# Moving the mLSTM gates behind the second projection, and opening two more products of the output projection at the mLSTM's end

## The chip, the cores and the metric

The kernel runs on one core of a Trainium2 chip. The metric is the device time of one execution in microseconds (us). Before the change it is 1308.25 us, the median of three runs from 1307.04 to 1308.48.

## The reference

One layer of an encoder over 512 tokens of width 1024, in float32:

- RMSNorm and one input projection, whose columns feed three mixers side by side: pooling with four windows; a bidirectional mLSTM with 4 heads of width 64; attention with 8 query heads and 2 key/value heads. Their outputs, 1024 columns together, go through one output projection and are added to x.
- In the mLSTM, q and k pass a convolution over 5 tokens and a SiLU. Each token has an input gate and a forget gate per head and direction. Running sums of the log forget gates and running maxima give decays; a head's scores q k are multiplied by the decays, and the values are summed with them. The two directions are added, normed per head and multiplied with a sigmoid of another projection.
- RMSNorm, then cross-attention (4 heads) into 256 memory tokens, added to x.
- RMSNorm, then 16 experts with SwiGLU, each taking its 64 best tokens, added to x; a last RMSNorm.

## The kernel before

The 512 tokens stand as 4 tiles of 128 (t = 0 to 3), the 1024 columns as 8 blocks of 128. A float32 product outside the experts is made from three faster ones: both factors are split into a high and a low part (`split`, L129 to L136: ScalarE casts the high part, VectorE or GpSimd subtracts), and `mm3` (L124 to L127) issues high x high, high x low and low x high. So a projection block with 8 steps is 24 products.

PSUM has eight banks, used by name: three for "mm", one for "oo", two for "tr" (transposes) and two for "sc" (scores). A name's banks go round in the order in which the program asks for them: a tile waits until the tile that held its bank has been read.

Work is written as generators that yield a cost after each piece. `weave(chain, filler, ratio)` (L161) emits a piece of the chain, multiplies its cost by the ratio, and emits pieces of the filler until that is paid; `run` emits what is left. This gives the order of the program. The framework then places the instructions (it is built with `schedule_with_timeline_sim=True`), and each engine executes its own queue in the order so found, which can differ from the order of the program where operands are ready earlier.

Stages around the change, in order:

1. The first half of attention (heads 0 to 3, `att_0`) is woven with two projections ("og", "vo"). Then `turn` (L355) transposes the queries of the second half.
2. The second half, `attention(4, 8)`, is the chain of a weave at ratio 1.0, and `fill_m` (L580) is its filler: the projection "mq" with its convolution, the load of "pl" (`load_w(7)`), `gates()`, the projection "mk" with its convolution, the decays of head 0 in both directions, the load of "k0" (`load_w(8)`). The attention chain has 21.2 units of cost, "mq" and "mk" 10.24 each.
3. `gates` (L593 to L639) works on tiles of 32 columns. It takes five "mm" tiles: one for the running sums (L610 to L612), two for transposes of `az` (L628), read by scans on VectorE (L630, L632), and two to turn the scans back (L636), read at L637. `az` lies in memory that the first half of attention used; GpSimd clears it at L622. `decay` takes one "mm" tile (L656), which ScalarE reads four times (L659).
4. `mlstm` is the chain of the next weave, at ratio 1.4, with `fill_kv` as its filler: the pool projection "pl", the pooling, the keys and values of the cross-attention ("k0", "k1", "v0", "v1"), and then three tiles of the output projection: (0,0), (1,0) and (0,1), as (token tile, half of the columns). These three take the "mm" banks and are held open: six of their eight steps are issued (`korder[:6]`), because the last two need the mLSTM's output. The filler has 44.0 units in all, the chain 31.9. At the end of head 1 and of head 3 stands a norm, a row of VectorE instructions (L760 to L765) with one on ScalarE; `out_turn` (L706) then turns two heads' result and splits it for the output projection.
5. `out_proj(0)` finishes the tiles of t = 0 and 1, adding each to x (L913): the held ones with their last two steps, (1,1) with all eight. `out_proj(1)` does t = 2 and 3 as the filler of the cross-attention's queries. The weights of these queries are split (L135, L136) into memory that is free after the turn.
6. The cross-attention, the routing and the experts follow. Each of the 16 experts has 24 MB of weights, read in pieces by `issue` into every arena of SBUF that the earlier stages have freed.

Of the kernel before, what the change touches and what calls it, by code (L numbers as in the profile page):

```python
# [98 lines left out]
def build(nc, tc, A, out, ne=NE, dbg=None):  # L99
# [21 lines left out]
    def SC():  # L121
        return ps.tile([128, 512], F32, name="sc")
# [91 lines left out]
    def load_w(i, parts=2):  # L214

        if i >= len(plan):
            return
        name, src, c0, n = plan[i]
        hb, lb = wring.next(), wring.next()
        st = KT // parts  # L220
        for j in range(parts):
            a, b = j * st, (j + 1) * st
            rbuf = raw.next()
            SP.dma_start(rbuf.f[:, 0:st, :n], src[:, a:b, c0:c0 + n])
            split(rbuf.f[:, 0:st, :n], hb.f[:, a:b, :n], lb.f[:, a:b, :n], le=(G if j % 2 and i < 7 else V))
        W[name] = (hb, lb, n)
# [86 lines left out]
    def fm_chunk(w, done):  # L313
        hb, lb, _ = W[w]
        for blk in range(2):
            p = MM()
            for k in range(KT):
                bs = slice(blk * 128, (blk + 1) * 128)
                mm3(p, hb.r[:, k, bs], lb.r[:, k, bs], hT_h[k].r, hT_l[k].r, k == 0, k == KT - 1)
                yield 0.64  # L320
            done(blk, p)
# [77 lines left out]
    fill = fill_q2()  # L399
# [180 lines left out]
    def fill_m():  # L580
        yield from fm_chunk("mq", conv_done(0))
        load_w(7)
        gates()
        yield from fm_chunk("mk", conv_done(1))
        for d in range(2):
            early.append(decay(0, d, MM))
            yield 0.43
        load_w(8)


    gs = Wr = None
# [1 line left out]
    def gates():  # L593
        az = Wr.bufs[0].f[:, 0:1024].rearrange("p (t d c) -> p t d c", d=2, c=128)
        Mrow = [Wr.bufs[1].f[:, d * S:(d + 1) * S] for d in range(2)]
        fpre = gt.f[:, :, 8:16]
        ipre = gt.f[:, :, 0:8]
        nf, ef, lf, bc, ag, mt, em, of = (gs.f[:, i] for i in range(8))
        mk_ = nf
        V.tensor_scalar(nf, fpre, -1.0, None, op0=ALU.mult)  # L600
        V.tensor_tensor(nf, nf, fpre, op=ALU.min)
        C.activation(ef, nf, AF.Exp)
        C.activation(ef, ef, AF.Ln, bias=1.0)
        V.scalar_tensor_tensor(lf, fpre, 0.0, ef, op0=ALU.min, op1=ALU.subtract)

        p = MM()
        pb = p[:, :32].rearrange("p (t c) -> p t c", c=8)
        pc = p[:, 32:64].rearrange("p (t c) -> p t c", c=8)
        F_, B_ = slice(0, 4), slice(4, 8)
        T.matmul(pb[:, :, F_], tri.f[:, 0], lf[:, :, F_], start=True, stop=True)  # L610
        T.matmul(pb[:, :, B_], tri.f[:, 1], lf[:, :, B_], start=True, stop=True)
        T.matmul(pc, ones.f, lf, start=True, stop=True)  # L612
        G.memset(of[:, 0, F_], 0.0)
        G.memset(of[:, 3, B_], 0.0)
        V.tensor_copy(of[:, 1, F_], pc[:, 0, F_])
        V.tensor_copy(of[:, 2, B_], pc[:, 3, B_])
        for i in range(2):
            V.tensor_tensor(of[:, 2 + i, F_], of[:, 1 + i, F_], pc[:, 1 + i, F_], op=ALU.add)
            V.tensor_tensor(of[:, 1 - i, B_], of[:, 2 - i, B_], pc[:, 2 - i, B_], op=ALU.add)
        V.tensor_tensor(bc, pb, of, op=ALU.add)  # L620
        V.tensor_tensor(ag, ipre, bc, op=ALU.subtract)
        G.memset(az, 0.0)  # L622
        V.tensor_copy(az.rearrange("p t d (h z) -> p (t d) h z", z=32)[:, :, :, 0],
                      ag.rearrange("p t (d h) -> p (t d) h", d=2))
        for d in range(2):
            p = MM()
            for t in range(NT):
                T.transpose(p[:, t * 128:(t + 1) * 128], az[:, t, d], idn)  # L628
            if d == 0:
                V.tensor_tensor_scan(Mrow[d], z0, p, 0.0, op0=ALU.max, op1=ALU.max)  # L630
            else:
                V.tensor_tensor_scan(Mrow[d][:, ::-1], z0, p[:, ::-1], 0.0, op0=ALU.max, op1=ALU.max)  # L632
        for d in range(2):
            p = MM()
            for t in range(NT):
                T.transpose(p[:, t * 128:(t + 1) * 128], Mrow[d][:, t * 128:(t + 1) * 128], idn)  # L636
            V.tensor_copy(mk_[:, :, 4 * d:4 * d + 4], p.rearrange("p (t h z) -> p t h z", t=4, z=32)[:, :, :, 0])  # L637
        V.tensor_tensor(mt, mk_, bc, op=ALU.add)
        C.activation(em, mt, AF.Exp, scale=-1.0)  # L639
# [33 lines left out]
    fill = fill_1()  # L673
# [15 lines left out]
    fill = fill_m()  # L689
# [13 lines left out]
    def out_turn(blk):  # L703
        p = OO()
        for t in range(NT):
            T.transpose(p[:, t * 128:(t + 1) * 128], hsum.f[:, t, blk * 128:(blk + 1) * 128], idn)  # L706
        split(p, y_h[2 + blk].f, y_l[2 + blk].f)
        yield 0.43

    def mlstm():  # L710
        nxt = early
        for h in range(4):
            wts = nxt
            if h < 3:
                nxt = [decay(h + 1, d, OO) for d in range(2)]
            for st in range(NT):
                p = SC()
                mm3(p, kz_h[h].r[:, st * 128:(st + 1) * 128], kz_l[h].r[:, st * 128:(st + 1) * 128],
                    mq_h[h // 2].r, mq_l[h // 2].r, True, True)
                for d in range(2):  # L720
                    o, js = seg[d][st]
                    wa = wts[d].f[:, o:o + js.stop - js.start]
                    V.scalar_tensor_tensor(wa, p[:, js], 1.0 / 32.0, wa, op0=ALU.mult, op1=ALU.mult)
                yield 0.64
            yield 1.0
            for d in range(2):
                c = 4 * d + h
                p = TR()
                pv = p[:, :NT * 65].rearrange("p (t c) -> p t c", c=65)
                for t in range(NT):  # L730
                    src = [st for st in range(NT) if (st <= t if d == 0 else st >= t)]
                    for i, st in enumerate(src):
                        o, js = seg[d][st]
                        oo = o + t * 128 - js.start
                        T.matmul(pv[:, t], wts[d].f[:, oo:oo + 128], mv[st].f[:, h, :],  # L735
                                 start=(i == 0), stop=(i == len(src) - 1))
                    yield 0.21 * len(src)
                if h == 2 and d == 1:
                    yield from out_turn(0)
                m = mst.next()  # L740
                dn, rc = m.f[:, 0:4], m.f[:, 4:8]
                V.scalar_tensor_tensor(dn, pv[:, :, 64], -1.0, em[:, :, c], op0=ALU.mult, op1=ALU.max)
                V.tensor_tensor(dn, dn, pv[:, :, 64], op=ALU.max)
                V.reciprocal(rc, dn)
                rb_ = rc[:, :, None].to_broadcast([128, NT, 64])
                ho = hsum.f[:, :, h * 64:(h + 1) * 64]
                if d == 0:
                    V.tensor_tensor(ho, pv[:, :, 0:64], rb_, op=ALU.mult)
                else:
                    tb = htmp.next()  # L750
                    V.tensor_tensor(tb.f[:, :, 0:64], pv[:, :, 0:64], rb_, op=ALU.mult)
                    V.tensor_tensor(ho, ho, tb.f[:, :, 0:64], op=ALU.add)
            if h % 2 == 0:
                continue

            sq, y, tm = (nst.f[:, i, h // 2] for i in range(3))
            tb = htmp.next()
            ho, oh = (b.f[:, :, (h - 1) * 64:(h + 1) * 64] for b in (hsum, og))
            C.activation(tb.f, ho, AF.Square)
            V.tensor_reduce(sq, tb.f.rearrange("p t (h d) -> p (t h) d", d=64), axis=AX.X, op=ALU.add)  # L760
            mean_rsqrt(sq, y, tm, 64)
            V.scalar_tensor_tensor(tb.f.rearrange("p t (h d) -> p t h d", d=64), ho.rearrange("p t (h d) -> p t h d", d=64),
                                   0.5, y.rearrange("p (t h) -> p t h", h=2)[:, :, :, None].to_broadcast([128, NT, 2, 64]),
                                   op0=ALU.mult, op1=ALU.mult)
            V.tensor_tensor(ho, tb.f, oh, op=ALU.mult)  # L765
        yield from out_turn(1)


# [36 lines left out]
    korder = [4, 5, 6, 7, 0, 1, 2, 3]  # L805
    wo_h, wo_l, held = {}, {}, {}
# [71 lines left out]
            yield from out_part(t, c, held[t, c], korder[:6])  # L878

    fill = fill_kv()  # L880
    weave(mlstm(), fill, 1.4)
    run(fill)
    kvT_h, kvT_l = kv["k"]
    vca = kv["v"]
# [219 lines left out]
    fill = out_proj(1)  # L1104
# [33 lines left out]
    fill = fill_q()  # L1138
# [311 lines left out]
```

## Time and profile before

| What | us |
|---|---|
| median of three runs | 1308.25 |
| the profiled execution, its own time | 1307.97 |
| span of that execution, first to last instruction | 1306.3 |
| PE (TensorE matmul) busy | 1236.4 (95%) |
| VectorE (DVE) busy | 441.6 (34%) |
| ScalarE (ACT) busy | 272.2 (21%) |
| GpSimd (POOL) busy | 118.1 (9%) |

The mean granted clock of TensorE is 0.988. In the profile, busy time per slice shows two halves: up to about 400 us several engines work and the DMA engines are far from full; from then on to the end PE and the DMA engines are both at nine tenths or more. Busy PE time is modelled from pipelined matmuls, so that a busy PE is not PE at its peak, and shares over the whole span mix stages with different limits. They are read stage by stage in the rows below.

### The profile page before, as it was taken

What the parts mean: (1) busy time and instruction counts of PE and PEld (TensorE: products, weight loads), DVE (VectorE), ACT (ScalarE), POOL (GpSimd) and SP (SyncE); (2) the same over time, 40 slices, a digit from 0 to 9 for tenths busy, and PEclk for the clock granted to TensorE, in tenths of its full rate; (3) what the DMA queues carried; (4) which work ended last, traced back from release to release, by engine and by line L of the source; (5) the groups of instructions that cost most, each with busy time, mean ns of one, the idle gap of its engine ahead of it and who ended that gap; (6) DMA issues with size and microseconds to landing.
All of it is one profiled execution on the core that took longest, in us unless ns stands there. A gap on an engine that the chain in (4) does not pass through costs nothing.

```text
span 1306.3 us, 15428 instructions
## 1 busy us (share of the span) xinstructions
PE 1236.4 (95%) x6257; PEld 637.5 (49%) x6257; DVE 441.6 (34%) x1007; ACT 272.2 (21%) x577; POOL 118.1 (9%) x157
## 2 busy tenths in 40 slices
PE   9898999899989999999999999999999999999986
PEld 8874779688853443343343334334333433433333
DVE  5897777436750022121221221202113020211313
ACT  6565645324410000101001010000101000010113
POOL 5422442103100000000000000000000000000012
PEclk9999999899989999999999999999999999999998
DMA  8210124305869899999999999999999999999995
GB/s 289 85 50 33 49 70 142 116 33 227 334 240 392 359 427 429 427 424 428 424 428 426 425 428 426 424 427 427 425 428 426 424 427 427 425 425 428 426 407 192
DMA packets 59974, 432.73 MB, mean 331 GB/s; under 512 B 5120, under 2 KB 23168, under 8 KB 30848
## 3 DMA queue, kind: packets, MB, share of 16 engines
q1 hardware_dynamic: 59904, 431.76, 80.4%
q8 instruction: 49, 0.80, 0.2%
q14 instruction: 21, 0.17, 0.0%
HBM read 429.64 MB, written 2.10 MB: 331 GB/s over the span
## 4 chain that ended last, share of the span: by engine, by line
PE 75%; DMA 9%; DVE 9%; ACT 3%; issue 2%; SPq 0%; POOL 0%; DVEq 0%; ACTq 0%; POOLq 0%
PE mm L1294 24%; PE sc L1325 14%; PE oo L1294 8%; PE tr L1221 5%; PE mm L125 3%; PE mm L126 3%; PE mm L127 3%; DMA rb_f<-in_expert_w_gu 3%; DMA rq_f<-in_expert_w_gu 3%; DMA r2a_f<-in_expert_w_down 3%; PE tr L1249 2%; PE tr L1250 2%; PE oo L442 1%; DVE f_f L1259 1%; PE tr L735 1%
## 5 line engine op out<-in xcount | busy, mean ns | idle before, releaser
L1259 DVE SCALAR_TENSOR_TENSOR f_f<-tr,f_f 128x512 f32<-128x512 f32 x112 | 79.9, 747 | 114.4 <-PE tr L1250 113.8
L1294 PE MATMUL mm<-rq_f,rg_f 128*64 128x512 f32 x364 | 91.7, 618 | 2.3 <-DMA rq_f<-in_expert_w_gu 2.2
L1344 POOL TENSOR_SCALAR f_f<-f_f 128x128 f32<-128x128 f32 x8 | 3.8, 494 | 890.7 <-PE tr L1237 864.6
L1221 PEld LDWEIGHTS tr<-f_f,ex_f 128*128 128x128 f32 x512 | 61.0, 191 | 40.9 <-issue 21.3
L1294 PE MATMUL mm<-r_f,rg_f 128*64 128x512 f32 x312 | 77.0, 618 | 3.1 <-DMA r_f<-in_expert_w_gu 3.1
L133 DVE TENSOR_TENSOR rp_r<-sc,rp_r 128x512 fp32r<-128x512 f32 (+1 forms) x31 | 21.0, 681 | 169.2 <-ACT rp_r L132 169.2
L1221 PE MATMUL tr<-f_f,ex_f 128*128 128x128 f32 x512 | 69.8, 284 | 7.1 <-ACT rg_f L1228 4.6
L1306 ACT ACTIVATE fb_f<-mm 128x512 f32<-128x512 f32 x32 | 19.0, 597 | 271.4 <-PE mm L1294 271.4
L1307 DVE TENSOR_TENSOR fb_f<-mm,fb_f 128x512 f32<-128x512 f32 x16 | 11.1, 692 | 176.6 <-PE mm L1294 170.5
L1228 ACT ACTIVATE rg_f<-tr,f_f 128x128 f32<-128x128 f32 x32 | 11.8, 368 | 281.2 <-PE tr L1221 209.3
L1249 PE MATMUL tr<-rp_r 128*128 128x512 f32 (+1 forms) x132 | 60.0, 459 | 8.9 <-DVE f_f L1259 7.4
L1226 DVE TENSOR_SCALAR rg_f<-tr,f_f 128x128 f32<-128x128 f32 x32 | 11.2, 351 | 157.6 <-PE tr L1221 111.7
L132 ACT CAST rp_r<-sc 128x512 fp32r<-128x512 f32 (+1 forms) x31 | 17.8, 579 | 184.8 <-PE sc L1325 184.8
L1249 PEld LDWEIGHTS tr<-rp_r 128*128 128x128 f32 x132 | 24.4, 187 | 64.4 <-DVE f_f L1259 26.5
L1250 PE MATMUL tr<-rp_r 128*128 128x512 f32 (+1 forms) x132 | 52.4, 403 | 2.3 <-DVE rp_r L133 0.9
L1325 PE MATMUL sc<-rq_f,fb_f 128*64 128x512 f32 x240 | 54.2, 595 | 0.2 <-DMA rq_f<-in_expert_w_down 0.2
L1294 PEld LDWEIGHTS mm<-rq_f,rg_f 128*64 128x64 f32 x364 | 24.5, 134 | 51.2 <-issue 45.5
L1294 PE MATMUL mm<-rb_f,rg_f 128*64 128x512 f32 x192 | 48.9, 619 | 0.0
L127 PE MATMUL mm<-r_r,rb_r 128*128 128x256 f32 (+2 forms) x160 | 46.6, 296 | 0.0
L126 PE MATMUL mm<-r_r,ra_r 128*128 128x256 f32 (+2 forms) x152 | 43.4, 289 | 0.8 <-POOL r_r L133 0.8
L125 PE MATMUL mm<-r_r,ra_r 128*128 128x256 f32 (+2 forms) x152 | 43.3, 295 | 0.4 <-ACT rq_f L372 0.4
L1325 PE MATMUL sc<-r_f,fb_f 128*64 128x512 f32 x192 | 43.4, 594 | 0.0
(460 smaller groups left out, 2274.6 us busy)
## 6 DMA issues: line engine op xcount, KB each, us to landing
r_f<-in_expert_w_gu SPq DMA_DIRECT2D x26, 2048.0 KB, 22.9
rq_f<-in_expert_w_gu SPq DMA_DIRECT2D x26, 2048.0 KB, 23.3
f_f<-in_expert_w_gu SPq DMA_DIRECT2D x13, 2048.0 KB, 23.0
r2a_f<-in_expert_w_gu SPq DMA_DIRECT2D x13, 2048.0 KB, 24.9
r_f<-in_expert_w_down SPq DMA_DIRECT2D x12, 2048.0 KB, 28.5
ra_f<-in_expert_w_gu SPq DMA_DIRECT2D x12, 2048.0 KB, 26.7
rb_f<-in_expert_w_gu SPq DMA_DIRECT2D x12, 2048.0 KB, 28.0
rq_f<-in_expert_w_down SPq DMA_DIRECT2D x12, 2048.0 KB, 30.3
```

What stands on the lines that cost most here:

```text
L125: T.matmul(o, lh, rh, start=start, stop=False)
L126: T.matmul(o, lh, rl, start=False, stop=False)
L127: T.matmul(o, ll, rh, start=False, stop=stop)
L132: C.copy(h.bitcast(F32R), src)
L133: (le or V).tensor_tensor(l.bitcast(F32R), src, h, op=ALU.subtract)
L1221: i = T.matmul(o, x.f[:, t, kt * 128:(kt + 1) * 128], flat(g.f[:, t]), start=(t == 0), stop=(t == NT - 1))
L1249: T.matmul(pp[:, i * w:(i + 1) * w], GT.r[:, ts_], flat(yh.r)[:, cs], start=True, stop=False)
L1250: T.matmul(pp[:, i * w:(i + 1) * w], GT.r[:, ts_], flat(yl.r)[:, cs], start=False, stop=True)
L1259: V.scalar_tensor_tensor(ao, p, g, ao, op0=ALU.mult, op1=ALU.add)
L1294: T.matmul(pg[2 * half + b][64 * ab:64 * ab + 64], xs.f[:, k, el * 64:(el + 1) * 64], wv[:, ab], start=(k == 0), stop=(k == KT - 1))
L1306: C.activation(hsl.f[:, b], pg[b], AF.Silu)
L1325: T.matmul(py[c][64 * ab:64 * ab + 64], hT.f[:, blk, 64 * ab:64 * ab + 64], wv[:, ab, c * 512:(c + 1) * 512], start=(blk == 0), stop=(blk ...
```

## The change

`fill_m` issues "mk" and the load of "k0" ahead of the gates, and yields 2.0 units between the gates and the decays. At the end of `mlstm`, ahead of the last `out_turn`, two more tiles of the output projection, (1,1) and (2,0), are opened in the "sc" banks and six of their eight steps issued; `out_proj` then finds them in `held`. The ratio of the weave of `mlstm` goes from 1.4 to 1.7.

```diff
     def fill_m():
         yield from fm_chunk("mq", conv_done(0))
         load_w(7)
+        yield from fm_chunk("mk", conv_done(1))
+        load_w(8)
         gates()
-        yield from fm_chunk("mk", conv_done(1))
+        yield 2.0
         for d in range(2):
             early.append(decay(0, d, MM))
             yield 0.43
-        load_w(8)
...
             V.tensor_tensor(ho, tb.f, oh, op=ALU.mult)
+        for t, c in ((1, 1), (2, 0)):
+            held[t, c] = SC()
+            yield from out_part(t, c, held[t, c], korder[:6])
         yield from out_turn(1)
...
     fill = fill_kv()
-    weave(mlstm(), fill, 1.4)
+    weave(mlstm(), fill, 1.7)
     run(fill)
```

## Rows read from the trace of the kernel before

**Rows 1.** Busy time by stretch: us, busy us (instructions) per engine, clock, DMA share, GB/s.
```profile
500.00:900.00 400.00, 390.79 (x1772) 147.19 (x1770) 82.11 (x145) 34.69 (x64) 0.00 (x0) 1.00 1.01 426
...
96.70:128.30 31.60, 24.93 (x121) 13.13 (x120) 24.40 (x59) 17.88 (x44) 8.02 (x8) 0.95 0.10 34
...
147.00:176.00 29.00, 28.28 (x148) 20.54 (x147) 19.92 (x40) 18.54 (x41) 12.96 (x17) 1.00 0.16 55
176.00:237.00 61.00, 61.00 (x429) 54.13 (x428) 43.93 (x97) 28.33 (x49) 23.88 (x35) 1.00 0.36 115
237.00:246.80 9.80, 9.80 (x58) 8.25 (x57) 4.23 (x14) 2.22 (x3) 2.55 (x2) 1.00 0.00 0
...
252.70:259.00 6.30, 6.30 (x14) 4.55 (x15) 5.22 (x8) 3.39 (x6) 0.00 (x0) 0.51 0.90 368
...
263.40:298.60 35.20, 35.20 (x209) 31.10 (x208) 9.84 (x26) 6.32 (x13) 0.00 (x0) 1.00 0.09 31
```

**Rows 2.** Timeline of the DMA queue on SP: start us, us, line.
```profile
299.73 15.04 SPq L498 DMA_DIRECT2D r_f<-in_expert_w_gu  x2
```

**Rows 3.** Timeline of PE around the end of attention's first half: start us, us, line.
```profile
95.88 0.29 PE L610 MATMUL mm<-f_f 128*128 128x16 f32 x2
...
101.59 5.34 PE L442 MATMUL oo<-f_f,rq_f 128*64 128x512 f32 x14 [0.69 <-ACT f_f L435]
...
118.60 3.65 PE L442 MATMUL oo<-f_f,rq_f 128*64 128x512 f32 x14 [0.29 <-ACT f_f L435]
...
128.39 0.47 PE L125 MATMUL mm<-ra_r,r_r 128*128 128x512 f32 x1
```

**Rows 4.** Timeline of PE around the mLSTM's end.
```profile
240.97 2.79 PE L735 MATMUL tr<-rq_f,f_f 128*128 128x65 f32 x24
...
251.38 0.63 PE L706 MATMUL oo<-f_f,rq_f 128*128 128x128 f32 x4 [4.59 <-DVE rq_f L765]
252.69 0.80 PE L125 MATMUL mm<-rc_r,rb_r 128*128 128x512 f32 x1 [0.68 <-ACT rb_r L132]
253.28 0.63 PE L126 MATMUL mm<-rc_r,rb_r 128*128 128x512 f32 x1
253.71 0.63 PE L125 MATMUL mm<-rc_r,rb_r 128*128 128x512 f32 x1
...
261.31 0.39 PE L125 MATMUL mm<-r_r,ra_r 128*128 128x512 f32 x1
261.54 0.39 PE L126 MATMUL mm<-r_r,ra_r 128*128 128x512 f32 x1
```

**Rows 5.** Timeline of the gates and decays, with the last transposes of attention.
```profile
118.26 0.95 POOL L622 MEMSET rq_f<- 128x1024 f32 x1 [1.10 <-PE tr L355]
...
129.09 0.15 DVE L637 COPY f_f<-mm 128x16 f32<-128x16 f32 x1
...
143.66 1.03 PE L656 MATMUL mm<-f_f 128*128 128x128 f32 x8
...
176.44 0.60 PE L432 MATMUL tr<-f_f,fb_f 128*128 128x128 f32 x4
```

**Rows 6.** Timeline of VectorE and GpSimd: splits (L133) and the rotation of queries (L344).
```profile
95.91 1.21 DVE L133 TENSOR_TENSOR r_r<-rq_f,r_r 128x1024 fp32r<-128x1024 f32 x1
...
85.10 0.41 DVE L344 TENSOR_TENSOR rq_f<-rq_f 128x256 f32<-128x256 f32 x1
85.51 2.55 DVE L344 TENSOR_TENSOR rq_f<-rq_f 128x256 f32<-128x256 f32 x1
...
83.19 4.59 POOL L133 TENSOR_TENSOR r_r<-rq_f,r_r 128x1024 fp32r<-128x1024 f32 x1 [0.18 <-ACT r_r L132]
145.69 3.37 POOL L133 TENSOR_TENSOR r2a_r<-fb_f,r2a_r 64x512 fp32r<-64x512 f32 x2 [0.29 <-ACT r2a_r L132]
```

**Rows 7.** Timeline behind the mLSTM: last split of the query weights, first cross-attention score.
```profile
261.88 2.74 DVE L136 SCALAR_TENSOR_TENSOR rq_r<-fb_f,f_f,rq_r 128x512 fp32r<-128x512 f32 x4 [3.91 <-ACT rq_r L135]
...
298.61 0.28 PE L125 MATMUL sc<-ra_r,rq_r 128*128 128x256 f32 x1
```

## The prediction

> **What bounds the kernel now.** I read the view of busy time by stretch first. From 500 to 900 us the expert stage keeps the DMA engines at a share of 1.01 and 426 GB/s with PE busy too [rows 1]: this part is a stream of weights whose length the change doesn't touch. Its buffers are memory that the stages before it free, and the first large group of them is issued only at 299.73 [rows 2]; from 263.4 to 298.6 the DMA share is 0.09 [rows 1]. So a microsecond won on PE before 299 lets the stream start a microsecond earlier, and I count it 1:1.
>
> Ahead of 299 PE is full (61.00 of 61.00 from 176 to 237, 35.20 of 35.20 from 263.4 to 298.6) but for two places. (A) From 96.7 to 128.3 it is busy 24.93 of 31.60, 6.67 idle, at a mean clock of 0.95 [rows 1]. Of two equal groups of 14 products of the first attention half, one took 5.34 and one 3.65 [rows 3], so the low clock cost 1.69 there. A holds 8.36 us. (B) At the mLSTM's end PE waits 4.59 for the last VectorE product of the norm (L765), turns the result, and then waits 0.68 for the ScalarE copy [rows 4]. The granted clock then falls: 0.51 from 252.7 to 259 [rows 1], that is the 1.2 GHz level, with products 0.43 apart (253.28, 253.71) in place of 0.23 (261.31, 261.54) [rows 4]. Of those 6.3 us, 6.3 x (1 - 0.23/0.43) = 2.9 are lost. B holds 4.59 + 0.68 + 2.9 = 8.2 us.
>
> The reason for A is in the order of tiles. "mm" tiles share three banks, handed out in program order. The sums of the gates (L610) run at 95.88, as "mq" ends, and the first product of "mk" only at 128.39 [rows 3]: "mk" stands behind the five tiles of the gates, and these wait for memory that the first attention half still uses (az is cleared at 118.26, once the turns at L355 have read what lies there, and the last copy runs at 129.09 [rows 5]). So PE has no independent products for 32 us.
>
> **The change part by part.**
>
> *Mk ahead of the gates.* Nothing is added: 48 products at 0.23, 11.0 us, now take their banks right behind "mq" and can go into the holes of A. They hold more than its 6.67 idle. Of VectorE the products need one read per block (L546) to free a bank. Most that this can give is 8.36, plus the 0.72 that PE is idle from 147 to 176 [rows 1]: 9.1. What it costs: "pl", the next filler, now stands behind the gates' five tiles as well as the decays' two. Were the gates done at the same time (129.24) and "mk" used up at about 124, PE would have attention alone for 5 us; attention alone loses 8.36 of 31.6, or 26% [rows 1, 3], so 1.3. The gates are now issued behind the convolution of "mk" and nearly all of the second attention half (the filler emits them after 20.5 of the 21.2 units of the chain, before after 10.2), so VectorE takes them later where both are ready; I let that make the hole 13 us, 3.4 us lost. I take 8.4 - 3.4 = 5.0. The other end is that the hole grows until attention is over, priced below.
>
> *The load of k0 ahead of the gates.* The gates issue no transfers, so the SP queue keeps its order. ScalarE's and VectorE's splits of k0 come as soon as "mk" is done, before the decays rather than behind them; VectorE is idle 7.2 of the 31.6 us of A [rows 1]. Zero; without that room, up to the two such splits, 1.21 each [rows 6], in the gates' chain, 2.4.
>
> *The pause of 2.0 units.* It issues nothing; it lets two units of attention, if any are left, be emitted ahead of the decays. Zero either way, since the decays are needed only by the mLSTM.
>
> *Two held products.* Tiles (1,1) and (2,0), 6 of 8 steps of 3 products: 36 x 0.23 = 8.3 us leave the output projection behind the turn and stand ahead of it. Their banks are the two "sc" banks, whose next user is the cross-attention at 298.61 [rows 7], after both tiles are added. Their last two steps wait for the turn as for the other three held tiles, but the step of y's third block can run too: another 6 products, 1.4 us. So 9.7 us of work meets a gap of 4.59 + 0.68, and the cover suffices if at least 5.3 of the 9.7 are left at the gap.
>
> *The ratio 1.7.* The filler has 44.0 units and the chain 31.9; at 1.4 they end together (44.7), at 1.7 the filler is gone after 25.9, among the scores of head 3. What it did in the last 5.6 units of the chain the new products must now do. From 237, where the last scores run, to the turn at 251.38 it is 14.4 us, of which PE works 9.8 [rows 1, 4]. Now 20 small products of head 3 (24 took 2.79 [rows 4], so 2.3), 9 products of step six on the three older tiles (2.1) and the 9.7 above fill 14.1. That is just enough. I take the gap and the low clock as gone and leave the 0.68, because the turn may queue behind a product: 4.59 + 2.9 = 7.5. Bounds 0 (all used up before the gap) and 8.2.
>
> *What is late next.* The query weights of the cross-attention are split into memory that the turn frees; the last pair's VectorE step runs 261.88 to 264.6 [rows 7], 13 us behind the turn. Moving PE up by 7.5 asks for them earlier, but the 78 products left in the second half of the output projection (18 us) don't need them. Zero; if that cover were gone, up to the 4 us between about 260 and 264.6. First expert buffer: it waits on L765, not on PE; zero.
>
> **Sum.** -5.0 - 7.5 = -12.5 against the profiled execution's 1307.97 (span 1306.3 and 1.67 around it, 0.28 below the median of the runs, 1308.25): 1295.5.
>
> **The rivals.**
>
> 1. *VectorE and GpSimd take A back.* Of two VectorE instructions of one line (L344) the one that began while GpSimd ran a 4.59 us split took 2.55, the one just before 0.41 [rows 6]. The GpSimd splits of "mk" (3.37 for two, 6.7 for both blocks [rows 6]) now run beside the softmax of the first attention half, whose every step passes VectorE. Against it: the splits come at the end of the convolution of "mk", when that half may be nearly done. If 5 of the 6.7 land on its path, A is worth nothing: 1307.97 - 7.5 = 1300.5. The Trainium skill, "SBUF — State Buffer", section "SBUF: two separate sides", says that VectorE instructions with two operands in that memory and GpSimd instructions share a pair of ports as a lock held for a whole instruction. By that rule each split shuts VectorE out for its length, and the trace agrees in the 2.55 us; this rival is what it gives here.
>
> 2. *The gap stays.* With the older filler gone early, the 36 products go into the holes of head 3 and PE again stands before the turn: 1307.97 - 5.0 = 1303. For it: 14.1 against 14.4 has no margin. Against it: PE had no holes from 176 to 246, so there is little for them to go into earlier.
>
> 3. *The gates come behind attention (slower).* Place: the "mm" banks between "mk" and "pl". If VectorE serves the gates only once attention is through, "pl" and all behind it are shut out, the second half of attention runs as bare as the first (another 8.4 lost, all of A), and then the gates' chain, 118.26 to 129.24 or 11.0 us [rows 5], stands with PE next to empty, followed by some 6.3 us of low clock as in B, 2.9. Net 8.4 - 8.4 + 11.0 + 2.9 - 7.5 = +6.4: 1314.4. It is slower than before once more than 7.5 of those 13.9 are exposed. Against it: before, the decays were emitted at the same late point, and PE ran them at 143.66, with transposes of attention still to come at 176.44 [rows 5], so instructions are placed by readiness and not by their place in the program alone.
>
> 4. *Neither counts*, the idle time turning up again in the projection or at the weights' loads: within 2.6 us of 1308.
>
> **How the numbers follow.** Forecast 0.52 (1290 to 1300), rival 1 0.18 (1298 to 1304), rival 2 0.10 (1300 to 1306), rival 3 0.12 (1310 to 1317), rival 4 0.08. Both bounds full give 1307.97 - 9.1 - 8.2 = 1290.7; a clock that stays up elsewhere could add a little, so the range begins at 1289. It ends at 1307, leaving out rival 3 and half of rival 4, about 0.16, and 0.04 below. What a measurement can tell from no change is 0.2%, 2.6 us: faster than 1305.6 is 0.52 + 0.18 + 0.08 of rival 2 = 0.78; within it 0.02 of rival 2, the 0.08 of rival 4 and 0.01 of rival 3, 0.11; slower than 1310.9 the other 0.11.
>
> **What would show it.** In the profile after: products of "mk" (mm <- ra, r) start just behind "mq" near 96, and PE's idle time up to 128 is under 3; "pl" starts before 137. Around the mLSTM's end the wait of L706 for L765 is under 1 and the stretch behind it has clock 1.00. The first cross-attention score comes near 286 and the first large expert buffers near 287. I am wrong on A if "mk" still starts behind the gates or a new hole lies between the last of "mk" and the first of "pl"; on B if the wait on L765 is still above 3; on the 1:1 if the score at 298.6 moves by 10 and the end doesn't.

## The result, and the profile after

The changed kernel takes 1300.0 us against 1307.64 for the kernel before, measured beside it: a ratio of 0.9941, 95% interval [0.9923, 0.9958]. That is 7.6 us faster; 12.5 were forecast. The profiled span is 1298.9 (before 1306.3).

The busy time by stretch of the changed kernel, with the columns of [rows 1] (us, then busy us and instructions of PE, PE's weight loads, VectorE, ScalarE, GpSimd; clock, DMA share, GB/s):

```profile
66.00:96.70 30.70, 30.02 (x165) 25.60 (x166) 27.87 (x72) 19.83 (x51) 8.76 (x10) 0.94 0.18 53
96.70:128.30 31.60, 25.86 (x127) 18.18 (x125) 30.17 (x59) 19.08 (x40) 10.31 (x9) 0.95 0.21 67
128.30:147.00 18.70, 17.35 (x89) 11.20 (x88) 11.45 (x28) 10.30 (x30) 7.38 (x13) 0.90 0.01 1
147.00:176.00 29.00, 26.73 (x136) 18.02 (x135) 17.98 (x39) 16.79 (x38) 3.47 (x5) 1.00 0.07 20
176.00:237.00 61.00, 61.00 (x427) 53.94 (x426) 42.61 (x95) 28.55 (x50) 22.41 (x36) 1.00 0.37 123
237.00:252.00 15.00, 15.00 (x90) 13.11 (x89) 6.49 (x20) 1.63 (x2) 2.55 (x2) 1.00 0.01 1
252.00:260.00 8.00, 7.33 (x35) 5.87 (x33) 4.34 (x16) 1.27 (x3) 0.00 (x0) 1.00 0.29 84
240.00:500.00 260.00, 251.99 (x1364) 160.66 (x1364) 96.97 (x302) 57.67 (x131) 16.32 (x23) 0.99 0.73 293
```

From 237 to 260 PE is idle 0.67 in all and the clock is 1.00: stretch B is mended. From 96.7 to 128.3 PE is still idle 5.74 at the same mean clock of 0.95, and VectorE is now busy 30.17 of 31.60 (24.40 before [rows 1]). Stretch A has not been won: where PE lacked work before, VectorE is now nearly full.

PE's timeline of the changed kernel (start, us, line; the brackets hold the idle time before and its releaser), at the places of [rows 3, 4, 7]:

```profile
115.98 0.29 PE L611 MATMUL mm<-f_f 128*128 128x16 f32 x2
...
125.78 1.94 PE L432 MATMUL tr<-f_f,fb_f 128*128 128x128 f32 x8 [4.46 <-DVE f_f L621]
...
128.59 5.27 PE L442 MATMUL oo<-f_f,rq_f 128*64 128x512 f32 x14
...
141.79 0.48 PE L125 MATMUL mm<-ra_r,r_r 128*128 128x512 f32 x1
...
173.83 0.50 PE L125 MATMUL sc<-rc_r,r2a_r 128*128 128x512 f32 x1
...
258.73 0.60 PE L707 MATMUL oo<-f_f,rq_f 128*128 128x128 f32 x4
260.00 0.50 PE L125 MATMUL mm<-rc_r,rb_r 128*128 128x512 f32 x1 [0.68 <-ACT rb_r L132]
...
285.81 0.36 PE L125 MATMUL sc<-ra_r,rq_r 128*128 128x256 f32 x1
```

The gates' sums (L611) come 20 us later than in [rows 3], since the 48 products of "mk" have filled PE up to there, as meant. But the last product group of attention's first half starts at 128.59 in place of 118.60 [rows 3], behind a hole of 4.46, and takes 5.27 for the 14 products that took 3.65 (the clock from 128.3 to 147 is 0.90), "pl" starts at 141.79, and the mLSTM's first score (sc, 173.83) comes 2.9 later than before, where it stood at 170.95:

```profile
170.95 0.40 PE L125 MATMUL sc<-rc_r,r2a_r 128*128 128x512 f32 x1
```

The last turn (L707, L706 before) now has no wait where it had 4.59 [rows 4]. The 0.68 for the ScalarE copy stays, as forecast.

The end follows the weight stream. Before, the stretch from 240 to 500 read so:

```profile
240.00:500.00 260.00, 246.50 (x1313) 158.50 (x1314) 96.22 (x296) 56.97 (x130) 16.23 (x23) 0.97 0.69 282
```

282 GB/s became 293, which over 260 us is 2.9 MB more moved by 500; at the stream's 426 GB/s [rows 1] that is 6.7 us, and the span is 7.4 shorter. The same reckoning comes within about 1 us of the span in every run below. The first large expert buffer is issued 6.0 earlier than in [rows 2]:

```profile
293.70 0.46 SPq L498 DMA_DIRECT2D r_f<-in_expert_w_gu  x1
```

### The profile page after: what moved, and what is told of

It is laid out like the page before. It is cut to its first block, busy times and chain, and to the rows that moved or that the text cites. A ratio compares the mean times of both kernels' runs of the same rounds, so it can differ in the third digit from the quotient of the medians.

```text
span 1298.9 us, 15426 instructions
## 1 busy us (share of the span) xinstructions
PE 1233.4 (95%) x6257; PEld 636.8 (49%) x6257; DVE 441.3 (34%) x1007; ACT 271.3 (21%) x577; POOL 112.0 (9%) x157
## 4 chain that ended last, share of the span: by engine, by line
PE 69%; DMA 15%; DVE 11%; ACT 3%; issue 2%; SPq 0%; POOL 0%; DVEq 0%; ACTq 0%; POOLq 0%
PE mm L1298 22%; PE sc L1329 14%; PE oo L1298 7%; PE tr L1225 5%; DMA rb_f<-in_expert_w_gu 3%; PE mm L125 3%; DMA rq_f<-in_expert_w_gu 3%; DMA r2a_f<-in_expert_w_down 3%; DMA r2a_f<-in_expert_w_gu 3%; PE mm L127 3%; PE mm L126 3%; DMA rq_f<-in_expert_w_down 2%; PE tr L1253 2%; PE tr L1254 1%; PE tr L736 1%
## 5 line engine op out<-in xcount | busy, mean ns | idle before, releaser
L133 DVE TENSOR_TENSOR rp_r<-sc,rp_r 128x512 fp32r<-128x512 f32 (+1 forms) x31 | 21.1, 683 | 168.5 <-ACT rp_r L132 168.5
L126 PE MATMUL mm<-r_r,ra_r 128*128 128x256 f32 (+2 forms) x150 | 43.3, 293 | 1.1 <-POOL r_r L133 1.1
L1298 PEld LDWEIGHTS mm<-r_f,rg_f 128*64 128x64 f32 x312 | 20.9, 134 | 45.8 <-issue 38.6
```

Of the source, the lines that this page charges most:

```text
L126: T.matmul(o, lh, rl, start=False, stop=False)
L133: (le or V).tensor_tensor(l.bitcast(F32R), src, h, op=ALU.subtract)
L1298: T.matmul(pg[2 * half + b][64 * ab:64 * ab + 64], xs.f[:, k, el * 64:(el + 1) * 64], wv[:, ab], start=(k == 0), stop=(k == KT - 1))
```

## The experiments

The theory after the first look: the held products give the whole gain, and A fails because the convolution of "mk" (VectorE) now runs inside attention's first half and stands ahead of its softmax. Rivals: that GpSimd and VectorE shut each other out (rival 1, the lock), attention's own latency, or a gain that the ratio made. A tap is one step of the convolution, a VectorE instruction for one of the 5 tokens (L549 for the first, L551 for the others; counts of taps below are of L551). Each run is given as a ratio to the kernel before, measured beside it, with its 95% interval.

**The parts one by one.** The order of the gates alone, at the ratio 1.4 and without the held products:

```diff
-        gates()
         yield from fm_chunk("mk", conv_done(1))
+        load_w(8)
+        gates()
+        yield 2.0
...
-        load_w(8)
```

> The order of the filler alone (mk and the load of k0 ahead of the gates, the pause of 2.0), with no new held products and the ratio 1.4. Theory (the profile after: VectorE is busy 30.17 of 31.60 us from 96.7 to 128.3 in place of 24.40, and the first half of attention ends 10 us later): the 11 us of mk's products that PE gains are given back while softmax steps queue behind mk's convolution on VectorE, so A is worth 0: within 2 us of the kernel before. Rival (the forecast): A is worth 5, about 5 us faster, and it is the mLSTM's end that gave less than it seems. Second rival: the new place of the gates costs by itself and the held products hide it: 2 to 5 us slower.

Measured: 1309.07, ratio 1.0018 [1.0009, 1.0027]. By itself this part makes the kernel 2.4 us slower: outside the theory's 2 us, in the range of the second rival. Its last turn still waits:

```profile
253.41 0.63 PE L707 MATMUL oo<-f_f,rq_f 128*128 128x128 f32 x4 [4.59 <-DVE rq_f L766]
```

The held products and the ratio, the gates where they were; then the held products alone:

```diff
-        yield from out_turn(1)
+        for t, c in ((1, 1), (2, 0)):
+            held[t, c] = SC()
+            yield from out_part(t, c, held[t, c], korder[:6])
+        yield from out_turn(1)
...
-    weave(mlstm(), fill, 1.4)
+    weave(mlstm(), fill, 1.7)
```

> The two held products and the ratio 1.7, with the filler's order as before. Theory: the whole gain of the change sits at the mLSTM's end, 4.59 of waiting, 2.9 of low clock: 7 to 8 us faster than before, the same as the whole change within 1.5. Rival (A gave something too): 2 to 5 us slower than the whole change.

> The two held products alone, the ratio still 1.4, the filler's order as before. Theory: the older filler ends with the chain, the 9.7 us of new products meet a gap of 5.3 and cover it: 7 to 8 us faster than before, PE's wait for the norm's last product under 1. Rival (the ratio is what moves the filler so that the cover fits): 3 to 4 us faster, with a wait of some 2 to 4 us left or a new one among the scores of head 3.

Measured: 1299.4, ratio 0.9945 [0.9931, 0.9958], with the ratio; 1300.63, ratio 0.9954 [0.9941, 0.9966], without it. The whole change (0.9941) can't be told from either. In the first of them the turn has no wait. Its mLSTM's first score stands at 170.50 and its first large expert buffer at 290.55, against 173.83 and 293.70 in the whole change. So in the traces the new order of the gates costs the whole change some 3 us as well; of these the spans show 1.4 (1297.5 and 1298.9), and the ratios nothing that can be told. Where the rest is made up, no run shows.

The ratio alone (only the last two lines of that diff):

> The ratio 1.7 alone, with no new held products and the filler's order as before. Theory: some 8 us of filler leave the last 5.6 units of the chain, nothing comes in their place, and PE's wait before the last turn grows from 4.6 to 7 to 11 us: 3 to 6 us slower than before. Rival (the ratio frees the chain to end sooner, whatever fills it): within 2 us of before.

Measured: 1307.48, ratio 1.0002 [0.9993, 1.0011], and the wait for the norm 5.3 in place of 4.6. I had expected a much longer wait and a loss; the wait is 0.7 longer and there is no loss. My reading, which no run tests by itself: the ratio orders what is emitted, and what is ready is placed anyway.

**What holds A.** First the convolution of "mk" cut short, in the changed kernel and in the held products with the ratio:

```diff
-            for w in range(1, 5):
+            for w in range(1, 1 if which else 5):
```

> The changed kernel, with the convolution of mk cut to its first tap (a part of the computation that is left out): 8 VectorE instructions of 0.75, 6.0 us, are gone from the middle of the first attention half. Theory (the VectorE queue, not the products' order, is what holds A: the first half's softmax stands behind the convolution): the first half's last group of L442 moves from 128.6 to near 123, and the time to 1295 to 1297, 3 to 5 under the changed kernel's 1300.0. Rival (A is held by the attention chain's own latency and the low clock): within 1 of 1300.

> The held products and the ratio with the gates where they were (1299.4), with the convolution of mk cut to its first tap, the same part left out. Here the convolution runs from 128 on, where PE is full (18.70 of 18.70). Theory: the 6.0 us of VectorE are worth nothing there: 1298.5 to 1300. Rival (VectorE bounds everything up to the mLSTM): 1294 to 1297, as much as in the changed kernel.

Measured: 1300.35, ratio 0.9944 [0.9931, 0.9956], and 1297.2, ratio 0.9920 [0.9907, 0.9934]. Both miss the theory; the first comes where the rival had put it. In the first, attention's first half does end earlier (its last group starts at 126.10, not 128.59) and the mLSTM's first score moves 3.3, from 173.83 to 170.53; but at the last turn 1.5 of it is left (257.24), PE being idle 1.52 in 176 to 237 where it was full, and at the end no gain can be told. In this run PE still has a hole of 3.15 ahead of 123.71: between the scores (118.4) and their maximum (120.02) VectorE runs a split of k0 (1.22) and the first tap (0.48), and on ScalarE the convolution's tanh (121.01) goes ahead of the exponential (121.54). So the rest of what follows "mk" and "k0" still stands in attention's way, and the run doesn't decide between theory and rival. In the second, some 2 us are won where I expected none; the trace shows 0.8 of it (first score 169.68, first large buffer 289.72), so VectorE is not quite free behind 128 either. How much of the VectorE time taken away reaches the end isn't its length.

Then the lock. GpSimd's four subtractions in the split of "mk" became ScalarE copies:

```diff
-                    split(a.f[pr], kz_h[2 * blk + i].f[pr], kz_l[2 * blk + i].f[pr], le=G)
+                    C.copy(kz_h[2 * blk + i].f[pr].bitcast(F32R), a.f[pr])
+                    C.copy(kz_l[2 * blk + i].f[pr].bitcast(F32R), a.f[pr])
```

> The changed kernel with GpSimd's four subtractions of the split of mk replaced by ScalarE copies (the low part then repeats the high part, so this split is left out of the computation). Theory (VectorE's own queue): these splits run at 116.8 to 119 and from 129, where they cost the softmax one instruction of 1.26 in place of 0.47: under 1 us, 1299 to 1300.5. Rival (the two engines lock each other out, and that is what took A back): 3 to 5 us faster, 1295 to 1297.

Measured: 1299.24, ratio 0.9936 [0.9924, 0.9949]; the first score of the mLSTM at 172.14, 1.7 earlier than in the changed kernel. At the end no difference can be told. ScalarE carries the copies in their place (busy 21.16 of 31.60 in A, 19.08 before that edit), so a little more may be in it. The splits cost something, and they are not what took A back.

Last the order on VectorE (called the late convolution below). All of the computation stays; the convolution of "mk", behind its read of the bank, is issued only after the last copy (L357) of the turns between the attention halves:

```diff
+            q = (C.copy if h % 2 else V.tensor_copy)(d.r[:, t * 128:(t + 1) * 128], p[:, h * 128:(h + 1) * 128])
+            if h % 2 == 0:
+                last_turn[:] = [q]
...
+            with tc.issue_after(last_turn[0].ins) if which else nullcontext():
+                a = cacc.next()
...
```

> The changed kernel, complete, with one order added: VectorE issues the convolution of mk (all behind its read of the bank) only after the last turn of the queries between the two attention halves. The products of mk still come ahead of the gates. Theory: A's holes are filled and the first half is not held up; VectorE has 15 of 18.7 us in 128 to 147 already, so a part comes back there: 1295.5 to 1298. Rival (the 12 us of VectorE cost the same wherever they stand among attention's steps): 1299.5 to 1301.

Measured: 1293.77, ratio 0.9893 [0.9877, 0.9908]: 13.3 us faster than before, 6 faster than the change, and faster than the theory's own range. This version beats both kernels. What is held back on VectorE is 8.4 us for the two blocks (0.49 + 4 x 0.75 + 0.69 each), not the 12 of the expectation. Its stretches:

```profile
96.70:128.30 31.60, 29.63 (x141) 19.24 (x140) 22.59 (x50) 17.46 (x38) 8.12 (x8) 0.95 0.24 67
128.30:147.00 18.70, 17.35 (x102) 14.32 (x101) 18.20 (x40) 11.87 (x31) 6.57 (x10) 1.00 0.00 1
...
240.00:500.00 260.00, 251.70 (x1353) 156.93 (x1354) 96.90 (x299) 58.27 (x133) 15.53 (x23) 0.99 0.76 303
```

VectorE's 30.17 in A are 22.59, PE's 25.86 are 29.63, and from 128.3 to 147 it is VectorE that is full. The mLSTM's first score comes 6.4 earlier than in the changed kernel, and the first large buffer 6.3 earlier:

```profile
167.39 0.40 PE L126 MATMUL sc<-rc_r,r2a_r 128*128 128x512 f32 x1
```

```profile
287.44 0.46 SPq L503 DMA_DIRECT2D r_f<-in_expert_w_gu  x1
```

By 500 it has moved 303 GB/s x 260 us, 5.5 MB more than the kernel before: 12.8 us at 426 GB/s, against 13.4 of span.

**The same order without the held products**, at the ratio 1.4:

> The late convolution without the held products and at the ratio 1.4, complete: mk ahead of the gates with its convolution behind the first attention half, and nothing else changed. Theory (A is worth some 5 to 6 us by itself once the convolution is out of the first half, and adds to what the held products give): the first mLSTM score some 3.5 earlier than before's 170.95, the wait for the norm still 4 to 5, and the time 1301 to 1302.5. Rival (won time ahead of the mLSTM's end is only waited away there as long as nothing covers it): 1304 to 1307.

Measured: 1303.46, ratio 0.9971 [0.9960, 0.9982], between the two. The first score moves by 4.8 (166.13), and so does the last turn, with its wait as long as before:

```profile
246.57 0.63 PE L713 MATMUL oo<-f_f,rq_f 128*128 128x128 f32 x4 [4.59 <-DVE rq_f L772]
```

So A can be had without B. The span is 4.7 shorter; the medians differ by 3.7. With the 7.2 of the held products and the ratio that makes 10.9 of the 13.3; the other 2.4 is about what the intervals leave open.

**How much the held products must cover.** One in place of two, on the late convolution:

```diff
-        for t, c in ((1, 1), (2, 0)):
+        for t, c in ((1, 1),):
```

> The late convolution with one held product (tile 1,1) in place of two, so that 18 + 3 products of 0.23, 4.85 us, are missing ahead of the last turn. By the prediction's sum (14.1 us of work for 14.4, no slack) all 4.85 come back as a wait, with some 2.9 of low clock behind it: 1298.5 to 1301.5. By the wait that the ratio alone left there (5.3 for the norm) one product of 4.85 already covers nearly all: wait under 1, the time within 1.5 of 1293.8.

Measured: 1301.52, ratio 0.9955 [0.9942, 0.9967], by the medians 7.75 slower than with two (8.1 by the ratios); the time is at the end of the range of the first reckoning and far from the other's. The wait and the low clock are both back, first in PE's timeline, then by stretch:

```profile
249.86 0.72 PE L713 MATMUL oo<-f_f,rq_f 128*128 128x128 f32 x4 [2.46 <-DVE rq_f L772]
```

```profile
237.00:252.00 15.00, 11.86 (x66) 9.82 (x65) 7.83 (x27) 3.07 (x5) 2.54 (x2) 0.94 0.13 34
252.00:260.00 8.00, 8.00 (x27) 6.16 (x26) 5.59 (x9) 2.94 (x6) 0.00 (x0) 0.68 0.83 332
260.00:298.60 38.60, 37.21 (x234) 32.94 (x233) 15.16 (x43) 12.74 (x30) 0.85 (x2) 1.00 0.20 67
```

Idle are 3.14 + 1.39; the clock costs 0.06 x 11.86 + 0.32 x 8.00 = 3.3. Together 7.8, where the version with two loses 0.97 in these stretches. But the wait is 2.46, not the 4.85 of the sum without slack. In the version with two, the norm's last product (VectorE) and the last turn (PE) stand so:

```profile
249.84 0.69 DVE L772 TENSOR_TENSOR rq_f<-rq_f 128x512 f32<-128x512 f32 x1
```

```profile
252.71 0.60 PE L713 MATMUL oo<-f_f,rq_f 128*128 128x128 f32 x4
```

The norm is ready at 250.53, so PE has 2.2 us of other work left there: a slack of 2.2, and 4.85 less it is near the wait of 2.46. The first reckoning had the right kind of loss and the wrong split of it.

**The ratio, and one more step.** The late convolution at the ratio 1.4, and, apart from it, with the first tap on ScalarE:

```diff
-            V.tensor_scalar(a.f, c.f[:, 0:S], cw[:, 0:1], None, op0=ALU.mult)
+            C.activation(a.f, c.f[:, 0:S], AF.Identity, scale=cw[:, 0:1])
```

> The late convolution with the ratio back at 1.4. Theory (the held products alone cover the end, the ratio only orders the filler): within 1 of 1293.8, no wait for the norm ahead of the last turn. Rival (the ratio is worth the 1.2 us by which the held products with it and without it differed): 1294.5 to 1295.5.

> The late convolution (1293.77), complete, with the first tap of all four convolutions of mq and mk as a ScalarE multiplication by the column in place of a VectorE one (four VectorE instructions of 0.49 to 1.51, about 2.8 us, leave; four of about 0.7 come to ScalarE, which is busy 17.5 of 31.6 us in the first attention half). Theory (VectorE's queue is still what holds attention from 85 to 150): 1 to 2.5 us faster, 1291.3 to 1292.8. Rival (attention's latency or the trip between the engines holds it now): within 1 of 1293.8.

Measured at 1.4: 1296.85, ratio 0.9921 [0.9909, 0.9933], some 3 us behind 1.7 (the intervals just don't meet), though neither waits at the last turn. The stretch that differs most is in the cross-attention, from 300 to 320. The first row is of the ratio 1.4, the second of 1.7:

```profile
300.00:320.00 20.00, 17.42 (x114) 15.59 (x113) 10.14 (x21) 7.73 (x23) 6.72 (x9) 1.00 0.65 242
```

```profile
300.00:320.00 20.00, 18.89 (x116) 16.79 (x116) 9.66 (x26) 8.99 (x28) 5.59 (x12) 1.00 0.89 343
```

PE idles 1.5 more and 2.0 MB less are moved in the 20 us. That the 3 us are lost there is not shown: by 500 the means are 300 and 303 GB/s, so all but 0.8 MB is made up. And with the gates and the convolution where they were, the same pair (the held products without and with the ratio) differs as much in this stretch, 193 against 314 GB/s, and by 0.0009 at the end, which can't be told apart.

Measured with the tap on ScalarE: 1295.89, ratio 0.9915 [0.9901, 0.9928], not faster and perhaps slower: a miss. The mLSTM's first score stands at 168.27, 0.9 later. What cost it stays open.

## Why the prediction was right and wrong

**B: right, in mechanism and size.** Of the 7.5 (4.59 + 2.9) the changed kernel has all: no wait, clock 1.00, and the 0.68 kept; alone, the held products and the ratio give 7.2. So the 7.6 measured is B, with nothing of the 5.0 forecast for A. "That is just enough" was a little too strict: in the changed kernel the norm is ready at 257.46 (VectorE, L766: 256.77 + 0.69) and the turn comes at 258.73, a slack of 1.3. That the cover must reach to there is borne out by the run with one held product, where 2.46 of the wait and 3.3 of low clock come back and the time is 7.75 longer. Rival 2 (the gap stays) is out.

**A: wrong.** The step that failed is "Of VectorE the products need one read per block (L546) to free a bank", and with it "I take 8.4 - 3.4 = 5.0": measured by itself, this part is not 5.0 faster but 2.4 slower. The read is all that the products need, but it makes the rest of the convolution ready, and VectorE runs that among attention's steps. In the changed kernel the groups of VectorE's instructions from 96.7 to 128.3 (line, shape, count, busy us, mean ns) hold 13 taps (8 + 5), 10.1 us, and four of the splits of 1.2:

```profile
L551 DVE SCALAR_TENSOR_TENSOR rq_f<-rq_f,f_f 128x512 f32<-128x512 f32 x8 | 6.3, 784 | 0.0
...
L133 DVE TENSOR_TENSOR r_r<-rq_f,r_r 128x1024 fp32r<-128x1024 f32 x4 | 4.9, 1215 | 0.0
L551 DVE SCALAR_TENSOR_TENSOR fb_f<-rq_f,f_f,fb_f 128x512 f32<-128x512 f32 x5 | 3.8, 758 | 0.0
```

Before there were five taps, 3.7 us, and two such splits:

```profile
L551 DVE SCALAR_TENSOR_TENSOR rq_f<-rq_f,f_f 128x512 f32<-128x512 f32 x4 | 2.9, 734 | 0.0
...
L133 DVE TENSOR_TENSOR r_r<-rq_f,r_r 128x1024 fp32r<-128x1024 f32 x2 | 2.4, 1215 | 0.0
...
L551 DVE SCALAR_TENSOR_TENSOR fb_f<-rq_f,f_f,fb_f 128x512 f32<-128x512 f32 x1 | 0.7, 743 | 0.0
```

That is 6.4 + 2.5 us more, eight taps and two splits, in a stretch where VectorE had 7.2 free. How it holds the softmax is seen in ScalarE's timeline, where the sum of the exponentials is read, and in VectorE's behind it:

```profile
121.21 0.19 ACT L419 ACTIVATION_READ_ACCUMULATOR fb_f<-sc,f_f 128x1 f32 x1
```

```profile
121.11 1.21 DVE L133 TENSOR_TENSOR r_r<-rq_f,r_r 128x1024 fp32r<-128x1024 f32 x1
...
123.58 0.74 DVE L551 SCALAR_TENSOR_TENSOR rq_f<-rq_f,f_f 128x512 f32<-128x512 f32 x1
124.23 0.15 DVE L420 RECIPROCAL f_f<-f_f 128x1 f32<-128x1 f32 x1
...
124.43 0.75 DVE L551 SCALAR_TENSOR_TENSOR rq_f<-rq_f,f_f 128x512 f32<-128x512 f32 x1
125.09 0.16 DVE L420 RECIPROCAL f_f<-f_f 128x1 f32<-128x1 f32 x1
125.16 0.47 DVE L424 TENSOR_SCALAR fb_f<-fb_f,f_f 128x512 f32<-128x512 f32 x1
125.55 0.18 DVE L621 TENSOR_TENSOR f_f<-mm,f_f 128x32 f32<-128x32 f32 x1
```

The sum is there at 121.40; its reciprocal (L420) runs at 124.23 and the scaling of the weights (L424), for which PE's transposes (L432, 125.78) wait, at 125.16. Of these 3.8 us two taps take 1.5 and a split of k0 0.9; the rest is attention's own copy and maximum and small steps of the gates. The wait is put down to L621, the last to end before it; the transposes read what L424 wrote. PE had its products and attention had lost its server: in the forecast VectorE was counted by its idle share, not by what would be queued ahead of whom. The late convolution shows that the rest of the step was sound: with the order on VectorE mended and nothing else, the whole change gives -13.3, near the -12.5 of the sum, and A by itself 3.7 of the 5.0.

**The load of k0: open.** Two more splits of weights are in the rows above, in a stretch that has no room, so the cover that I named for them was not there. One of them has 0.9 us of the 3.8 above. What they cost at the end no run separates; the late convolution has them there too.

**Rival 1: its number came, its price was another.** It put A's worth at nothing, 1300.5 against 1300.0. It named the GpSimd splits as the cause. While such a split runs, VectorE is slow indeed. The first row is of GpSimd, the second of VectorE:

```profile
116.82 2.69 POOL L133 TENSOR_TENSOR r2a_r<-fb_f,r2a_r 64x512 fp32r<-64x512 f32 x2 [2.78 <-ACT r2a_r L132]
```

```profile
117.10 1.26 DVE L424 TENSOR_SCALAR fb_f<-fb_f,f_f 128x512 f32<-128x512 f32 x1
```

1.26 stands against the 0.47 of the same line at 125.16. The pair of rows that rival 1 started from is weaker than it read: not only the L344 of 2.55 but also the one of 0.41, at 85.10, began inside the split of 83.19 to 87.78 [rows 6]. VectorE ran on for its first 2.3 us and only then stood, and a split of the same form took 2.52 at 62.50, so of the 4.59 some 2 may be GpSimd's own wait (an estimate). And with the splits of "mk" gone from GpSimd the time is 1299.24, 0.8 less than the changed kernel's, and the order on VectorE gives 6.2. The Trainium skill, "SBUF — State Buffer", section "SBUF: two separate sides", has the two engines' shared port pair held as a lock for a whole instruction; the 1.26 agrees with it, and the run without the splits says that here it is a small part.

**The ratio.** The prediction gave it no price of its own. Alone it does nothing that can be told; with the late convolution it is worth some 3 us, which the prediction didn't look for and whose cause stays open.

**What I said would show it.** "Mk" right behind "mq": yes. PE's idle time in A under 3: no, 5.74. "pl" before 137: no, 141.79; with the late convolution 136.09. The first cross-attention score near 286: 285.81, and still no sign of 12.5, for at the ratio 1.7 it stands earlier in PE's order (the held products have it at 291.68 with 1.4 and at 282.66 with 1.7, and their ends can't be told apart). The first large buffers, forecast near 287, came at 293.70, and they were the better sign: 6.0 earlier, 7.6 faster. Rival 3 had the right sign for this part alone, which is 2.4 slower where it reckoned 13.9 against A, and it named VectorE's late service of the gates; the decays came early all the same (140.09).

## What to carry to other kernels

When work is moved ahead to fill one engine's holes, count also what its results make ready on the other engines, and who stands behind that in their queues; an idle share of 23% is no room for a chain that passes the engine at every step. If the follow-up isn't needed soon, give it a place in that engine's order as well: here this turned nothing into 6 us. For a wait at the end of a stage, the cover must hold until what is waited for is ready: here, with one held product of two, a wait of 2.46 was left, the clock behind it fell to 0.68 for 8 us, and most of the loss was back.

## What was not expected of the hardware

PE can look full and not be at its peak. From 66 to 96.7 the kernel before is busy 28.76 of 30.70 at clock 1.00, and the held products with one tap 30.70 of 30.70 at 0.90, yet the products there end within 0.4 of each other (the gates' sums start at 95.88 and 96.23). What one profile shows as idle time (1.9), another shows as low clock (0.10 of 30.7, 3.1), so the two have to be added before stretches are compared.

A tiny copy behind the clearing of its memory (L624, 128x32) took 1.31 in the changed kernel, beside a GpSimd split of 2.60 for two, and 0.20 in the run with one tap. Such a delay lies inside an instruction's busy time, where no idle time tells of it.
